# A hybrid GLA and RWKV-7 layer on one core: the input projection by seven block products instead of eight, and the triangular inverses behind it

## The chip, the cores and the metric

The kernel runs on one core of a Trainium2 chip. The core's engines each work through a queue of their own, strictly in order: TensorE (PE in the profile, its weight loads PEld), VectorE (DVE), ScalarE (ACT), GpSimd (POOL) and SyncE (SP), which here only issues DMAs, nearly all of them. The time is the device time of one execution in microseconds (us), the median of the runs of a kernel on the same chip; lower is better.

## The reference, cut to what matters

One encoder layer over 2048 tokens of width 1024, all in float32:

```python
h   = x @ w_in                      # [2048, 1024] @ [1024, 3344]: the input projection
A   = GLA(h[:, :1552])              # q 256, k 256, v 512, gate 512, gate-rank 16
B   = RWKV7(token_shift(h[:, 1552:]))   # r, k, v 512 each, three low-rank inputs 64 + 64 + 128
gates = sigmoid(x @ w_merge + b_merge)  # [2048, 2 * 1024]
mix = (gates[0] * (A @ w_branch[0]) + gates[1] * (B @ w_branch[1])) @ w_out
x   = LN(alpha * x + mix)
x   = LN(alpha * x + relu(x @ W1 + b1)**2 @ W2 + b2)
```

The token shift mixes each projected RWKV column with the same column of the token before: `u + (prev - u) * mu`. GLA and RWKV-7 are recurrences over tokens; the kernel does both in chunks of 128 tokens. For RWKV-7 that takes, for every chunk and head, the inverse of a unit triangular 128x128 matrix, (I - A)^-1 with A made of products of two projected streams, alpha and beta.

## The kernel before, in words

**Stages.** The profiled execution runs through the input projection of the first 1024 tokens (0 to about 432 us), the same of the second 1024 (to about 868 us), 16 chunks of both recurrences (to about 1700 us), the merge and the output product (to about 2200 us) and the MLP (to the end). `HB` is 1024, a "half" of the sequence. A scheduler of the framework decides in which order the recorded instructions stand in each engine's queue: it goes by dependencies and by the order in which the program records them; `high_priority` shifts that.

**Dense products.** float32 is made of two float32r parts, hi (a cast, on ScalarE) and lo (source minus hi, on VectorE or GpSimd; `split`, line 170). Every product is three matmuls, hi by hi, hi by lo, lo by hi (`mm3`, lines 164 to 166). Weights come through four `raw` buffers of 128x1024 (`wslot`, line 155), the load of 512 KB, the cast and the subtraction all ahead of the product.

**Projection of a half** (`phase0`). The input lies in SBUF, channel by token, split (`XH`, `XL`). `gemm` makes 128 features by 1024 tokens from one weight tile: two PSUM tiles of 512 tokens with 8 channel tiles by 3 matmuls each. First come GLA values, one half of the columns token-major (`vpart(1)`: inputs stationary, 264 weight columns moving; the 16 gate-rank columns are among them), then the low-rank inputs, then four rounds j of three gemms (k, r, v of two RWKV heads), each with elementwise work behind it, on POOL the lines 452 (`f`), 465 (`be`) and 472 (`ka`). The log decays stay in SBUF as `lwh`, `lwl`, and a cumulative-sum product per round takes them from there. The products alpha, beta, and others go to DRAM (line 440).

**Inverses** (`tstage`, once per half). It loads alpha and beta of 8 chunks back (line 647), makes A by 64 matmuls (line 654), sends the diagonal 32x32 blocks to DRAM by 32 small DMAs (line 559) and back one block to a partition (`QZ`, line 560), inverts them in 30 steps of two DVE operations (lines 565, 567), sends them out and back (`qe`), transposes (line 669) and puts the 128x128 inverses together by small matmuls (`rwkv_t`). `tstage(h)` stands inside `phase0`, ahead of eight GLA gemms (q, k, gate) and `vpart(0)`, whose matmuls stand in PE's queue among and behind the inverses' own.

**Chunks** (`phase1`). Of each chunk a serial chain of small matmuls and evacuations; the first evacuation of each chunk is `R` (DVE, line 767). The merge gates, `gates(b)` for 512 tokens (16 weight tiles, 384 dense matmuls `pd<-GH,whi` and so on; lines 164 to 166), are recorded after chunks 3, 7, 11 and 15 at a priority by which they fill PE between the chunks' small products. For b > 0, and for b = 0 from the fifth weight tile on, their lo parts are made on POOL.

**MLP.** Its up product already goes by seven block products: sums of weight blocks on POOL (line 1216, `sum<-raw`), their lo parts on DVE (line 174, `wl<-sum,wh`).

## Time and profile before

| | |
|---|---|
| three runs | 3519.4, 3522.22, 3526.28 us |
| median | 3522.22 us |
| the profiled execution: span | 3521.8 us, 51325 instructions |
| PE busy | 95%, 19704 matmuls |
| DVE, ACT, POOL busy | 67%, 39%, 29% |

The profiled execution's span is its whole time as far as the profile shows it, 0.4 us under the median of the runs. The page gives busy times over the whole span; tables by stretch of time (windows) give them per stage, and the timeline gives single instructions with their start and length, and in brackets how long the engine had idled before and what released it.

### The profile page before, as it was taken

The numbers are of one execution on the slowest core, as the hardware profiler recorded it, in microseconds if no ns is written. First come the engines' busy times: TensorE is split into PE (matmuls) and PEld (weight loads), VectorE is DVE, ScalarE is ACT, GpSimd is POOL, SyncE is SP. The second block draws the span as 40 slices with busy tenths as digits, with TensorE's granted clock in tenths as the row PEclk, the third lists the DMA queues.
The fourth block names the chain that finished last, engine by engine and source line by source line (L and its number), as shares of the span: only waits on it lengthen the run. The fifth ranks groups of instructions, "written<-read, shape, count | busy, mean of one in ns | idle before, by whom it ended". The sixth has DMA issues, their size and how long they took to land.

```text
span 3521.8 us, 51325 instructions
## 1 busy us (share of the span) xinstructions
PE 3333.7 (95%) x19704; PEld 2858.3 (81%) x19704; DVE 2353.1 (67%) x3962; ACT 1377.3 (39%) x2504; POOL 1038.5 (29%) x722
## 2 busy tenths in 40 slices
PE   8999999997899999999999979999989999989997
PEld 6777867777778778777899978999978999978886
DVE  4774547556884746542455577677788667789888
ACT  3532444323333323332322235444444444444553
POOL 0120002102344435443233353222243222244333
PEclk8999999998999999999999989999999999999999
DMA  4335523446434434334444433211233221133222
GB/s 149 108 109 161 165 86 124 138 126 198 137 117 136 157 125 162 126 126 158 165 138 144 136 136 124 72 61 60 72 108 132 72 72 57 64 108 138 100 98 79
DMA packets 268438, 417.74 MB, mean 119 GB/s; under 512 B 52476, under 2 KB 163102, under 8 KB 268192
## 3 DMA queue, kind: packets, MB, share of 16 engines
q1 hardware_dynamic: 268192, 414.46, 35.4%
q8 instruction: 155, 2.54, 0.3%
q14 instruction: 91, 0.75, 0.1%
HBM read 310.57 MB, written 103.81 MB: 118 GB/s over the span
## 4 chain that ended last, share of the span: by engine, by line
PE 57%; DVE 13%; DMA 3%; issue 2%; ACT 2%; POOL 2%; SPq 0%; DVEq 0%; POOLq 0%; ACTq 0%
PE pd L166 11%; PE pd L165 11%; PE pd L164 11%; PE pa L164 5%; PE pa L166 5%; PE pa L165 5%; DVE Qz L854 2%; DVE wl L174 2%; DVE hl L174 1%; PE pa L862 1%; PE pa L743 1%; DMA raw<-in_wu 1%; DVE acc L1275 1%; POOL sum L1216 1%; DVE SC L865 1%
## 5 line engine op out<-in xcount | busy, mean ns | idle before, releaser
L1216 POOL TENSOR_TENSOR sum<-raw 128x512 f32<-128x512 f32 x248 | 350.5, 1419 | 891.6 <-DVE wl L174 744.8
L171 ACT CAST whi<-raw 128x1024 fp32r<-128x1024 f32 (+1 forms) x230 | 227.8, 990 | 822.9 <-PE pa L166 410.2
L1275 DVE TENSOR_TENSOR acc<-acc,pa 128x512 f32<-128x512 f32 x480 | 318.8, 681 | 150.2 <-PE pa L166 148.6
L164 PE MATMUL pa<-whi,hh 128*128 128x512 f32 x960 | 376.7, 393 | 12.0 <-DVE acc L1275 10.5
L165 PE MATMUL pa<-wlo,hh 128*128 128x512 f32 x960 | 376.0, 392 | 3.4 <-DVE wlo L174 3.4
L166 PE MATMUL pa<-whi,hl 128*128 128x512 f32 x960 | 375.2, 391 | 0.0
L174 DVE TENSOR_TENSOR wlo<-raw,whi 128x1024 fp32r<-128x1024 f32 (+1 forms) x170 | 204.4, 1202 | 129.1 <-ACT whi L171 102.1
L164 PE MATMUL pd<-XH,whi 128*128 128x512 f32 x704 | 286.2, 406 | 3.6 <-ACT whi L171 3.6
L166 PE MATMUL pd<-XH,wlo 128*128 128x512 f32 x704 | 284.8, 405 | 1.1 <-DVE wlo L174 1.1
L165 PE MATMUL pd<-XL,whi 128*128 128x512 f32 x704 | 283.4, 403 | 0.0
L174 DVE TENSOR_TENSOR wl<-sum,wh 128x512 fp32r<-128x512 f32 x240 | 195.8, 822 | 82.5 <-ACT wh L171 82.4
L164 PEld LDWEIGHTS pa<-whi,hh 128*128 128x128 f32 x960 | 180.7, 188 | 57.0 <-DVE acc L1275 18.6
L165 PE MATMUL pd<-GL,whi 128*128 128x512 f32 x512 | 220.3, 430 | 0.0
L164 PE MATMUL pd<-GH,whi 128*128 128x512 f32 x512 | 218.8, 427 | 0.0
L166 PE MATMUL pd<-GH,wlo 128*128 128x512 f32 x512 | 218.0, 426 | 0.1
L165 PEld LDWEIGHTS pa<-wlo,hh 128*128 128x128 f32 x960 | 181.1, 189 | 40.4 <-DVE wlo L174 4.0
L166 PEld LDWEIGHTS pa<-whi,hl 128*128 128x128 f32 x960 | 180.7, 188 | 38.4
L171 ACT CAST wh<-sum 128x512 fp32r<-128x512 f32 x240 | 148.4, 619 | 151.2 <-PE pd L165 106.0
L174 POOL TENSOR_TENSOR wlo<-raw,whi 128x1024 fp32r<-128x1024 f32 x60 | 152.3, 2538 | 171.4 <-ACT whi L171 171.4
L452 POOL TENSOR_SCALAR f<-th,dv 128x512 f32<-128x512 f32 x16 | 12.3, 770 | 553.5 <-ACT th L450 553.5
L164 PEld LDWEIGHTS pd<-XH,whi 128*128 128x128 f32 x704 | 135.1, 192 | 45.4 <-issue 9.8
L166 PEld LDWEIGHTS pd<-XH,wlo 128*128 128x128 f32 x704 | 135.1, 192 | 36.4 <-issue 2.8
(374 smaller groups left out, 8942.7 us busy)
## 6 DMA issues: line engine op xcount, KB each, us to landing
raw<-in_wu SPq DMA_DIRECT2D x96, 512.0 KB, 4.3
raw<-in_wd SPq DMA_DIRECT2D x96, 512.0 KB, 3.3
raw<-in_wm SPq DMA_DIRECT2D x64, 512.0 KB, 4.2
raw<-in_wf SPq DMA_DIRECT2D x44, 512.0 KB, 4.1
d_gt<-gt SPq DMA_DIRECT2D x64, 256.0 KB, 2.0
gl<-d_gt SPq DMA_DIRECT2D x58, 256.0 KB, 3.0
raw<-in_wv SPq DMA_DIRECT2D x32, 264.0 KB, 3.8
raw<-in_xT SPq DMA_DIRECT2D x16, 512.0 KB, 4.8
```

Source lines behind the costliest of these rows:

```text
L164: nc.tensor.matmul(ps, lhsT=lhs[0], rhs=rhs[0], start=first, stop=False)
L165: nc.tensor.matmul(ps, lhsT=lhs[0], rhs=rhs[1], start=False, stop=False)
L166: nc.tensor.matmul(ps, lhsT=lhs[1], rhs=rhs[0], start=False, stop=last)
L171: nc.scalar.copy(hi, src)
L174: getattr(nc, lo_eng).tensor_tensor(lo, src, hi.bitcast(F32), op=ALU.subtract)
L452: nc.gpsimd.tensor_scalar(f, th, self.ka1(j), self.ka2(j), op0=ALU.mult, op1=ALU.add)
L743: nc.tensor.matmul(both[q][:, j * 128:j * 128 + 128], lhsT=lh[r, j, :], rhs=rr[r, j, :], start=True, stop=True)
L854: nc.vector.tensor_tensor(Qz[r, :, 0:n, hh, :], E[r], q[r].unsqueeze(2).to_broadcast([64, 2, n, 128]), op=ALU.mult)
L862: nc.tensor.matmul(ps[:, j * 128:j * 128 + 128], lhsT=Kt[:, j, l - l0, :], rhs=rhs, start=True, stop=True)
L865: nc.vector.copy_predicated(dst, m, ps.rearrange("p (a n w) -> p a n w", a=4, w=h))
L1216: getattr(self.nc, eng).tensor_tensor(src, block(spec[0]), block(spec[1]), op=spec[2])
L1275: nc.vector.tensor_tensor(a, a, ps, op=ALU.add)
```

## The change

Per half, `phase0` now makes the projection by Strassen's scheme in Winograd's form.

- `load_x(h)` loads all 1024 tokens (16 DMAs of 256 KB) and builds seven input blocks of 4 channel tiles by 512 tokens, each as hi and lo: the quarters B11, B21, B22 and the sums T1 to T4. Per channel tile (four of them) that is 7 casts on ACT, 2 differences and 5 lo parts on DVE, 2 differences and 2 lo parts on POOL. One set of buffers (`XB`) serves both halves.
- `pair(p)` makes two feature tiles by 1024 tokens at a time. Of the two weight tiles' quarters (A11, A12, A21, A22) it forms s1 to s4, splits seven 128x512 blocks, and runs seven products of 4 channel tiles by 3 matmuls, each 512 columns. Outputs leave PSUM through sums with the temporaries p1, p5 and u3 and land in SBUF (`hb`, from which the token shift now reads). On POOL stand s1 to s4, one output, one addition to p5 and five of the seven lo parts: 11 operations of 128x512 for each pair; the lo parts of A12 and S1 and the other outputs are DVE's.
- 13 pairs per half: the low-rank inputs, then per j k with r and v with a GLA q or k tile, then the four gate and the four value tiles of GLA. The values are now feature-major, stored whole to `d_vg` and transposed per chunk by four matmuls and an ACT copy in `gla_prep`.
- The 16 gate-rank columns get 80 matmuls of their own, 512 columns each, over both halves.
- The log decays `lw` go to DRAM (2 MB a half) and come back, 512 KB ahead of each round j; the cumulative sum is one float32 matmul where two float32r ones stood.
- `tstage(h)` leaves `phase0`. `phase1` begins with `tstage(0)`, `gates(0)`, `tstage(1)`, `gates(1)`; the chunks' loop follows, with `gates(2)` after chunk 6 and `gates(3)` after chunk 13. The SBUF pools of weights are closed and opened anew between projection and chunks, and the DMA scratch size is set to 1024.

The diff, cut to its core:

```diff
+            halves("B11")
+            sub("T1", "B12", "B11", nc.vector)
+            halves("B21")
+            sub("T2", "B22", "T1", nc.gpsimd)
+            halves("T2", lo_eng="gpsimd")
+            halves("T1")
+            sub("B12", "B22", "B12", nc.vector)
+            halves("T3", "B12")
+            sub("B21", "T2", "B21", nc.gpsimd)
+            halves("T4", "B21", "gpsimd")
+            halves("B22")
...
-    def gemm(self, src, evac, lo_eng="vector"):
...
+    def pair(self, src, p, put, evs):
...
+        pool = nc.gpsimd
+        halves("A11", a11, "gpsimd")
+        pool.tensor_tensor(s1, a21, a22, op=ALU.add)
+        pool.tensor_tensor(s2, s1, a11, op=ALU.subtract)
+        halves("A12", a12, "vector")
+        p1 = temp("p1", None, prod("A11", "B11"))
+        out(0, 0, prod("A12", "B21"), p1)
+        evs[0](0)
+        halves("S2", s2, "gpsimd")
+        u2 = temp("p1", nc.vector, prod("S2", "T2"), p1, p1)
+        halves("S1", s1, "vector")
+        p5 = temp("p5", None, prod("S1", "T1"))
+        s3 = v3(self.wp.tile([128, 512], F32, tag="wsa", name="wsa", bufs=1))
+        pool.tensor_tensor(s3, a11, a21, op=ALU.subtract)
+        halves("S3", s3, "gpsimd")
+        u3 = temp("u3", nc.vector, prod("S3", "T3"), u2)
+        out(1, 1, u3, p5, eng=pool)
+        pool.tensor_tensor(p5, p5, u2, op=ALU.add)
+        halves("A22", a22, "gpsimd")
+        out(1, 0, u3, prod("A22", "T4"), ALU.subtract)
+        pool.tensor_tensor(s2, a12, s2, op=ALU.subtract)
+        halves("S4", s2, "gpsimd")
+        out(0, 1, prod("S4", "B22"), p5)
...
+        nc.sync.dma_start(sp["lw"][h], lw)
...
+            nc.sync.dma_start(lw, sp["lw"][h][:, :, j * 128:j * 128 + 128])
...
-        self.tstage(h)
...
+        pair(11, values(0), values(1))
+        pair(12, values(2), values(3))
+        if h + 1 < self.S // HB:
+            steps, xl_close = self.load_x(h + 1)
...
+        for h in range(self.S // self.HB):
+            self.tstage(h)
+            self.gates(h)
...
-            if c % 4 == 3:
+            if c in (6, 13):
                 with self.tc.high_priority(offset=0):
-                    self.gates(c // 4)
+                    self.gates(2 + c // 8)
```

Three places show how the order of the instructions moves. First PE, where the first half's inverses begin. In the kernel before, `L654 ... pa<-raw` are the products A of the inverses, and `pd<-XH,whi` and its two neighbours the dense matmuls of the projection:

```order
L418 MATMUL pa<-rkl,cr 128x512
L654 MATMUL pa<-raw 128x128 x12
L164 MATMUL pd<-XH,whi 128x512
L165 MATMUL pd<-XL,whi 128x512
L166 MATMUL pd<-XH,wlo 128x512
L654 MATMUL pa<-raw 128x128 x4
L164 MATMUL pd<-XH,whi 128x512
```

In the changed kernel the last matmuls of the last product of the second half, `pd<-XB22h,wh` and neighbours (block B22 by weight sum S4), stand ahead of the same products A (now line 755), and the merge gates, `pd<-GH,whi` and neighbours, behind them:

```order
L167 MATMUL pd<-XB22h,wh 128x512
L168 MATMUL pd<-XB22l,wh 128x512
L169 MATMUL pd<-XB22h,wl 128x512
L755 MATMUL pa<-raw 128x128 x64
L167 MATMUL pd<-GH,whi 128x512
L168 MATMUL pd<-GL,whi 128x512
L169 MATMUL pd<-GH,wlo 128x512
```

The products A, which stood between matmuls of the projection, now stand alone between the last dense matmul of the projection and the first of the gates. The inverse's later products of the first half stand behind 216 of the 384 matmuls of `gates(0)`; the second half's A stand behind all 384, and its later products behind 185 matmuls of `gates(1)`.

Second SP, at the same place. Before, the small DMAs `qd<-aab` are followed by stores of the projection's results (`d_qT<-gq`) and by its weight loads (`raw<-in_wf`):

```order
L647 DMA raw<-d_be_127 128x4x128
L559 DMA qd_2374<-aab 32x8x32 x19
L560 DMA QZ<-qd_2374 128x1024
L559 DMA qd_2374<-aab 32x8x32 x13
L512 DMA d_qT_150<-gq 128x512
L512 DMA d_qT_151<-gq 128x512
L155 DMA raw<-in_wf 128x1024
L560 DMA QZ<-qd_2374 128x1024
```

After, the 16 loads of alpha and beta stand behind the store of the projection's last output; `raw<-d_be_231` is the last of them, `raw<-in_xT` the gates' input and `raw<-in_wm` their weights:

```order
L748 DMA raw<-d_be_231 128x4x128
L656 DMA qd_6112<-aab 32x8x32 x18
L657 DMA QZ<-qd_6112 128x1024
L656 DMA qd_6112<-aab 32x8x32 x13
L723 DMA raw<-in_xT 128x512 x3
L657 DMA QZ<-qd_6112 128x1024
L723 DMA raw<-in_xT 128x512 x5
L158 DMA raw<-in_wm 128x1024 x6
```

What follows the `qd` DMAs is no longer stores and loads of products that have weights in hand, but the first loads of the products that come next.

Third POOL, in a round j of the projection. Before, the queue holds the elementwise lines of the RWKV tiles alone, six for each round:

```order
L452 TENSOR_SCALAR f<-th,dv 128x512
L472 TENSOR_TENSOR ka<-kp,Ei 128x512
L465 TENSOR_TENSOR be<-be,Ei 128x512
L452 TENSOR_SCALAR f<-th,dv 128x512
L472 TENSOR_TENSOR ka<-kp,Ei 128x512
L465 TENSOR_TENSOR be<-be,Ei 128x512
```

After, 22 operations of the pairs stand among them (line 177: lo parts; 364 and 383: an output and p5; 368, 369, 379, 386: s1 to s4; 536, 550, 556: the elementwise lines):

```order
L364 TENSOR_TENSOR hb<-u_1759,p_1738 128x512
L383 TENSOR_TENSOR p_1738<-p_1738,p_1651 128x512
L177 TENSOR_TENSOR wl<-wsb,wh 128x512
L386 TENSOR_TENSOR wsb<-raw,wsb 128x512
L379 TENSOR_TENSOR wsa<-raw 128x512
L536 TENSOR_SCALAR t_1810<-th,dv 128x512
L177 TENSOR_TENSOR wl<-wsa,wh 128x512
L368 TENSOR_TENSOR wsa<-raw 128x512
L177 TENSOR_TENSOR wl<-raw,wh 128x512
L556 TENSOR_TENSOR o<-kp,Ei 128x512
L550 TENSOR_TENSOR o<-o,Ei 128x512
```

A round's queue on POOL grows from 6 operations to 28, and weights of the next products (line 177) stand behind the elementwise lines of the current ones.

More of the change, by code (lines that the diff above doesn't have):

```diff
@@ new lines, in wraw, with halves, prod, temp @@
+    def wraw(self, src, p):
+        raw = [self.raw() for _ in range(2)]
+        for x in range(2):
+            self.nc.sync.dma_start(raw[x], src[2 * p + x])
+        return [r.rearrange("p (k f) -> p k f", k=8) for r in raw]
+    def pair(self, src, p, put, evs):
+        nc = self.nc
+        raw = self.ahead.pop(0) if self.ahead else self.wraw(src, p)
+        a11, a12, a21, a22 = (raw[a][:, 4 * k:4 * k + 4, :] for a in range(2) for k in range(2))
+        v3 = lambda t: t.rearrange("p (k f) -> p k f", k=4)
+        s1, s2 = (v3(self.wp.tile([128, 512], F32, tag=t, name=t, bufs=1)) for t in ("wsa", "wsb"))
+        W = {}
+        def halves(n, t, lo_eng):
+            hi, lo = (v3(self.wp.tile([128, 512], F32R, tag="w" + x, name="w" + x, bufs=4)) for x in "hl")
+            self.split(t, hi, lo, lo_eng=lo_eng)
+            W[n] = hi, lo
+        def prod(w, x):
+            ps = self.pd()
+            for k in range(4):
+                self.mm3(ps, tuple(t[:, k, :] for t in W[w]), tuple(t[:, k, :] for t in self.XB[x]), k == 0, k == 3)
+            return ps
+        def temp(tag, eng, x, y=None, out=None):
+            t = self.T.tile([128, 512], F32, tag=tag, name=tag, bufs=1) if out is None else out
+            if y is None:
+                nc.scalar.copy(t, x)
+            else:
+                eng.tensor_tensor(t, x, y, op=ALU.add)
+            return t
+        def out(a, b, x, y, op=ALU.add, eng=nc.vector):
+            eng.tensor_tensor(put(a, b), x, y, op=op)
+        pool = nc.gpsimd
[21 more added lines that the diff above has]
+        out(0, 1, prod("S4", "B22"), p5)
+        evs[0](1)
+        evs[1](0)
+        evs[1](1)
@@ L427, in phase0 @@
                 for d in range(2):
-                    for i, part in enumerate((lwh, lwl)):
-                        nc.tensor.matmul(ps[:, d, 0:130], lhsT=part[:, c + d, j * 128:j * 128 + 128], rhs=self.cumM, start=i == 0, stop=i == 1)
+                    nc.tensor.matmul(ps[:, d, 0:130], lhsT=lw[:, c + d, :], rhs=self.cumM, start=True, stop=True)
                 nc.scalar.activation(Ex[:, c:c + 2, :], ps[:, :, 0:129], AF.Exp, scale=-DECAY)
@@ L520, in phase0 @@
-        for j in range(4):
-            def ev_g(n, ps, j=j):
-                t = T.tile([128, 512], F32, tag="gth", name="th")
-                nc.scalar.activation(t, ps, AF.Tanh, scale=0.5)
-                q = T.tile([128, 512], F32, tag="gq", name="gq")
-                nc.vector.scalar_tensor_tensor(q, t, 1.0, ps, op0=ALU.add, op1=ALU.mult)
-                nc.sync.dma_start(sp["ug"][b0 + n][:, j, :], q)
-            gemm(A["wf"][18 + j], ev_g)
-        vpart(0, T, ("gq", "gth"), lambda n: self.load_x(h + 1, 0) if n == 0 and h + 1 < self.S // HB else None)
+        T2, t2close = self.pool(f"p0g_{h}", bufs=2)
@@ new lines, in values, with put @@
+        def values(i):
+            ts = {}
+            def put(b):
+                ts[b] = T2.tile([128, 512], F32, tag="gx", name="gx", bufs=4)
+                return ts[b]
+            return put, lambda n: nc.sync.dma_start(sp["vg"][b0 + n][:, i, :], ts[n])
+        pair(9, gates(0), gates(1))
+        pair(10, gates(2), gates(3))
+        pair(11, values(0), values(1))
+        pair(12, values(2), values(3))
+        if h + 1 < self.S // HB:
+            steps, xl_close = self.load_x(h + 1)
+            for f in steps:
+                f()
+            xl_close()
@@ L529, in phase0 @@
+        t2close()
         tclose()
@@ L828, in gla_prep @@
         ug = self.ld("ug", c, [128, 4, 128], 1)
-        vg = self.ld("vg", c, [128, 512])
+        gv = self.ld("vg", c, [128, 4, 128], 1)
+        pv = self.pa()
+        for j in range(4):
+            nc.tensor.transpose(pv[:, j * 128:j * 128 + 128], gv[:, j, :], self.ident)
+        vg = T.tile([128, 512], F32, tag="vgt", name="vgt", bufs=2)
+        nc.scalar.copy(vg, pv)
         qk = T.tile([128, 2, 128], F32, tag="qk", name="qk", bufs=1)
```

310 lines of the change are left out of this document (151 added, 159 removed).

## The prediction

> **What bounds the kernel now.** I read the page's busy shares and its chain first, then windows by stage. Of the page, the busy line and the chain by engine:
>
> ```profile
> PE 3333.7 (95%) x19704; PEld 2858.3 (81%) x19704; DVE 2353.1 (67%) x3962; ACT 1377.3 (39%) x2504; POOL 1038.5 (29%) x722
> PE 57%; DVE 13%; DMA 3%; issue 2%; ACT 2%; POOL 2%; SPq 0%; DVEq 0%; POOLq 0%; ACTq 0%
> ```
>
> TensorE bounds the whole. The stages that the change touches, as windows (window, its length, then busy time of PE, PEld, DVE, ACT, POOL with counts, granted clock, DMA share, GB/s): the two halves of the projection, the chunks, the start, and the step from projection to chunks.
>
> ```profile
> 0.00:432.00 432.00, 406.94 (x2552) 321.63 (x2553) 250.82 (x378) 170.62 (x312) 39.06 (x37) 0.96 0.44 136
> 432.00:868.00 436.00, 405.13 (x2579) 318.26 (x2578) 258.43 (x400) 167.46 (x315) 56.81 (x49) 0.95 0.44 135
> 868.00:1700.00 832.00, 786.18 (x5055) 657.95 (x5055) 482.08 (x1056) 264.84 (x420) 339.75 (x205) 0.99 0.42 136
> 0.00:44.00 44.00, 32.34 (x206) 30.73 (x207) 21.23 (x37) 18.93 (x27) 0.20 (x4) 0.92 0.73 239
> 836.00:880.00 44.00, 26.73 (x195) 24.45 (x194) 32.76 (x60) 17.23 (x29) 21.45 (x18) 0.77 0.75 232
> ```
>
> The projection loses only 25 and 31 us of PE's time. POOL is nearly free there (39 and 57 us): that slack, and the inverses hidden beside gemms, are what the change spends.
>
> **Matmuls.** Their price is the spacing of starts, since busy times overlap. Timeline of PE, nine matmuls of 512 columns from the first row to the second, six of 264 from the third to the fourth; then the group of the chunks' transposes of values; then two DVE instructions one round j apart:
>
> ```profile
> 202.01 0.39 PE L165 MATMUL pd<-XL,whi 128*128 128x512 f32 x1
> 204.12 0.40 PE L165 MATMUL pd<-XL,whi 128*128 128x512 f32 x1
> 423.90 0.29 PE L166 MATMUL pd<-whi,XL 128*128 128x264 f32 x1
> 424.64 0.29 PE L166 MATMUL pd<-whi,XL 128*128 128x264 f32 x1
> ```
> ```profile
> L732 PE MATMUL pa<-cf,ld_vT 128*128 128x128 f32 x64 | 11.5, 282 | 5.2 <-DMA ld_vT<-d_vT 5.2
> ```
> ```profile
> 179.66 0.17 DVE L432 COPY e<-Ex 128x8 f32<-128x8 f32 x1 [0.23 <-ACT Ex L430]
> 221.89 0.17 DVE L432 COPY e<-Ex 128x8 f32<-128x8 f32 x1 [0.23 <-ACT Ex L430]
> ```
>
> 2.11 / 9 = 0.234 us, 0.74 / 6 = 0.124 us. Before: 2 halves x 22 gemms x 48 = 2112 of the first and 2 x 2 x 192 = 768 of the second. After: 26 pairs x 7 x 12 = 2184, and 80 for the gate ranks. So 2264 - 2112 = 152 more of the first (+35.6) and 768 fewer of the second (-95.2): -60. The values' transposes, 64 of the shape in the group's row, add 11.5; the gate ranks' 16 go, at most a quarter of that: -3. The cumulative sums trade two cheap matmuls for one float32 one: zero, a microsecond or two either way. **PE's work: -52**, certain by the counts; all else is what PE waits.
>
> A round now is 42.2 us: 144 x 0.234 = 33.8, and 8.5 of small products and waits. After, it has 168 dense matmuls: 39.4 + 8.5 = 47.9 (it takes in a GLA tile, so it is longer, not slower).
>
> **The start.** PE's first matmul, and the loads of the input:
>
> ```profile
> 6.30 1.25 PE L164 MATMUL pd<-whi,XH 128*128 128x264 f32 x4 [6.30 <-ACT whi L171]
> ```
> ```profile
> raw<-in_xT SPq DMA_DIRECT2D x32, 256.0 KB, 2.9
> ```
>
> Before, `vpart` starts on quarters of the input, and 44 us lose 44 - 32.3 = 12 us. After, the first pair's last two products need T4 and B22 of all four channel tiles, behind 4 MB of loads and 1 MB of weights (22 us at the window's 239 GB/s) and behind POOL's 16 and DVE's 28 operations on the input, which (next part) largely exclude each other: 16 x 1.31 + 28 x 0.68 = 40 us, beside the pair's own sums. The pair so ends between 50 us (the 40 beside the loads) and 69 (behind them, with the last products), and holds 84 x 0.234 = 20 us of matmuls: 30 to 49 lost, less the 12 lost before: 18 to 37. I take **+20**, near the small end, since each channel tile's operations start when its four loads are there.
>
> **The low-rank part.** Stores and loads of 512 KB land in 4 us:
>
> ```profile
> raw<-in_wm SPq DMA_DIRECT2D x64, 512.0 KB, 4.2
> ```
>
> A 2 MB store, then the first 512 KB back, stand ahead of the first cumulative sum, and PE, in order, waits behind it: some 5 us a half: **+10** for both (0 to 20).
>
> **POOL beside DVE in the rounds.** POOL's elementwise groups, and the MLP's three instructions that show the price, the second started while the first ran, the third alone:
>
> ```profile
> L452 POOL TENSOR_SCALAR f<-th,dv 128x512 f32<-128x512 f32 x16 | 12.3, 770 | 553.5 <-ACT th L450 553.5
> L465 POOL TENSOR_TENSOR be<-be,Ei 128x512 f32<-128x512 f32 x16 | 28.2, 1760 | 4.8 <-issue 4.8
> L472 POOL TENSOR_TENSOR ka<-kp,Ei 128x512 f32<-128x512 f32 x16 | 25.1, 1569 | 26.2 <-DVE kp L454 26.2
> ```
> ```profile
> 2904.67 1.31 POOL L1216 TENSOR_TENSOR sum<-raw 128x512 f32<-128x512 f32 x1 [0.88 <-DMA raw<-in_wu]
> 2905.25 1.28 DVE L174 TENSOR_TENSOR wl<-raw,wh 128x512 fp32r<-128x512 f32 x1 [1.91 <-ACT wh L171]
> 2907.85 0.68 DVE L174 TENSOR_TENSOR wl<-sum,wh 128x512 fp32r<-128x512 f32 x1
> ```
>
> The DVE subtraction takes 0.68 alone; started 0.58 after POOL's sum it ends at 2906.53, 0.55 after POOL's end (2905.98). It got nothing done while POOL read SBUF, but for 0.13 us of entry. So the two queues add up: per round POOL holds 22 x 1.31 + 2 x (0.77 + 1.76 + 1.57) = 37.0 us; DVE has 26 operations with two SBUF inputs (4 lo parts of weights, 22 elementwise ones) of 0.55 to 0.68, 14.3 to 17.7. Together 51.3 to 54.7; I take 53 against PE's 47.9: 5.1 x 8 rounds = **+41**. Bounds: 0 where PE still covers it, 81 where DVE becomes the bound (rival below). The skill's page "SBUF — State Buffer" ("Who interferes with whom") says that a VectorE instruction with two SBUF inputs contends with a GpSimd one that reads SBUF and fully blocks for the whole of it. By that rule every DVE operation costs its full 0.68 behind POOL, the round is 54.7 and the term +54; the trace's 0.55 says somewhat less.
>
> **Between the halves.** The second half's input blocks have one set of buffers: T2, T4 and their lo parts wait on POOL behind the first half's last pair, and the next first product on those. Like the start, but loads come ahead: **+10** (0 to 20).
>
> **The inverses.** SP's queue and PE in the first half's inverses; landing times of the gates' 256 KB and the weights' cast; DVE's steps on `QZ` (the first and the last) and the transposes behind them; the lo parts on POOL; the windows that hold the first and the second half's `qd`:
>
> ```profile
> 272.73 0.63 SPq L647 DMA_DIRECT2D raw<-d_be  x1
> 273.45 11.10 SPq L559 DMA_DIRECT2D qd<-aab  x19
> 285.11 7.09 SPq L559 DMA_DIRECT2D qd<-aab  x13
> ```
> ```profile
> 274.07 3.47 PE L654 MATMUL pa<-raw 64*128 64x128 f32 x32 [0.19 <-ACT aab L655]
> ```
> ```profile
> L171 ACT CAST whi<-raw 128x1024 fp32r<-128x1024 f32 (+1 forms) x230 | 227.8, 990 | 822.9 <-PE pa L166 410.2
> d_gt<-gt SPq DMA_DIRECT2D x64, 256.0 KB, 2.0
> ```
> ```profile
> 306.60 0.26 DVE L565 TENSOR_TENSOR qtmp<-QZ 128x60 f32<-128x60 f32 x1
> 344.01 0.22 DVE L567 TENSOR_TENSOR QZ<-QZ,qtmp 128x60 f32<-128x60 f32 x1
> 358.62 1.30 DVE L669 STREAM_TRANSPOSE tn<-tt 128x512 f32<-128x512 f32 x2
> ```
> ```profile
> L174 POOL TENSOR_TENSOR wlo<-raw,whi 128x1024 fp32r<-128x1024 f32 x60 | 152.3, 2538 | 171.4 <-ACT whi L171 171.4
> ```
> ```profile
> 264.00:308.00 44.00, 39.51 (x206) 32.14 (x207) 5.56 (x10) 11.52 (x20) 0.00 (x0) 0.90 0.72 183
> 704.00:748.00 44.00, 41.52 (x170) 32.72 (x169) 32.41 (x55) 8.02 (x11) 0.00 (x0) 0.96 0.46 155
> ```
>
> Before, these windows lose 4.5 and 2.5 us: gemms with weights in hand ran while SP spent 11.1 + 7.1 = 18.2 us on issuing `qd`. After, nothing dense is in hand. From the last Strassen product to the first gate matmul stand, one after another: the output's store (2.0), 16 loads of alpha and beta (0.63 each: 10) and the last one's landing (2.9), the last A and its copy (1), `qd` (18.2) and its landing, for which SP's `QZ` load waits (2), eight loads of `in_xT` (0.5 each: 4), `in_wm` (4.2) and its cast (1): 45 us, in which PE has 64 products A, 7 us. 38 idle. At the second, the loads of four chunks come ahead and no store is waited for: 45 - 7 = 38, 31 idle. 38 + 31 - 7 = **+62** (50 to 72). Nothing fills it: PE's queue holds A alone between `XB22` and `GH`.
>
> Then the inverse's later products. Before, from the last A (277.5) to the transposes (358.6) went 81 us, the DVE steps 37.6 of them, with POOL at 0.00. After, PE's idle 38 and 216 gate matmuls (51 us) stand against that in the first, 31 and 185 (43) in the second: 8 short at the second, and gate splits now run on DVE, and POOL's lo parts of 2.54 us hold off the steps, whose inputs both lie in SBUF. **+15** for both (0 to 35).
>
> **The chunks.** Their start has now gates beside it: of the window 836 to 880, 17 us idle, go: **-17**. The pace, from `R` of a chunk to the next, with 24 gate matmuls between the first two rows, and 191 between the others:
>
> ```profile
> 945.35 0.68 DVE L767 COPY R<-pa 128x512 f32<-128x512 f32 x1
> 980.01 0.68 DVE L767 COPY R<-pa 128x512 f32<-128x512 f32 x1
> 1062.40 0.69 DVE L767 COPY R<-pa 128x512 f32<-128x512 f32 x1 [4.51 <-PE pa L765]
> 1138.83 0.69 DVE L767 COPY R<-pa 128x512 f32<-128x512 f32 x1 [2.27 <-PE pa L765]
> ```
>
> 34.7 and 76.4 us: (76.4 - 34.7) / 167 = 0.25 a matmul, 0.016 over its price; half of the 1536 gate matmuls leave the chunks and run dense: some **-9** (0 to -12).
>
> **Sum:** -52 + 20 + 10 + 41 + 10 + 62 + 15 - 17 - 9 = **+80**, on 3521.8 (0.4 under the runs' median): **3602 us**. With the port term kept, the other terms' bounds drawn half-way give 3570 to 3635.
>
> **Rivals.**
> *PE hides all that POOL and DVE do* (faster). It decides where POOL's operations hold DVE off for under 1.1 us, or DVE slips between them, so that a round stays within PE's time. Then the port's 41, the 15 of late inverses, 15 of the start's and the 10 between the halves go. Besides, outputs now go through SBUF, so a round could lose its waits of today, which this window, about one round long, shows:
>
> ```profile
> 88.00:132.00 44.00, 40.61 (x184) 31.51 (x184) 32.28 (x39) 28.22 (x47) 7.33 (x6) 0.96 0.24 81
> ```
>
> 3.4 us x 8 = 27. 108 in all: 3522 + 80 - 108 = 3494. For it: DVE is only 59% busy in the projection, and tiles are buffered. Against it: 1.31 in POOL's row, and the 37 of 48 us that POOL alone would fill. 0.20.
> *DVE in its order becomes the bound* (slower still). Its own work in a round, scaled from the projection's 509 us over 868, with the outputs' sums in the evacuations' place, is some 34 us; with waits on POOL's operations and on ACT and PE it could take 58 instead of 53: 5 x 8 = +40: 3642. For it: an in-order queue hardly fills every gap. 0.22.
> *It cancels out*: a port term near zero and the inverses at their small end leave about zero to +20. 0.10, of which 0.06 within 0.2% (7 us, the spread of the three runs, and about what a measurement of this kernel can tell from no change).
> That the change does not do what it says is excluded by the order: 12 matmuls a product, 7 products a pair.
>
> **How the numbers follow.** The forecast has 0.48; slower = 0.48 + 0.22 + 0.04 = 0.74, same 0.06, faster 0.20. The range goes from the first rival, 3490, to 3660, past the second with its own few us.
>
> **What would show it.** Right: PE idle about 38 and 31 us between the last `XB22` and the first `GH`, and between the two blocks of gates; rounds j of 51 to 55 us, with DVE's two-input operations ending 0.55 after POOL's; the first pair ending past 50 us. Wrong: rounds at 48 us or less, or dense matmuls inside the issue of `qd`.

## The result, and the profile after

The changed kernel takes 3686.01 us (median; 3684.01 to 3687.84) against 3524.25 in the same set of runs: 1.046 times as long, 95% interval 1.0444 to 1.0475, or +162 us. The forecast was +80. The profiled execution has a span of 3681.9 us, +160. Of all runs below, one execution, of the kernel with the input blocks on DVE, took 5969.92 us at a granted clock of 0.84; it is left out. The page:

```profile
span 3681.9 us, 50968 instructions
PE 3333.9 (91%) x19136; PEld 2828.4 (77%) x19136; DVE 2559.2 (70%) x4030; ACT 1448.9 (39%) x2672; POOL 1496.5 (41%) x1040
```

PE is busy for as long as before (3333.7), with 568 fewer recorded matmuls; all that is new is waiting, and matmuls that run slowly. The windows that answer to those of before, and then the start, a stretch of three rounds, and the way from the projection to the chunks:

```profile
0.00:432.00 432.00, 360.32 (x1342) 256.84 (x1342) 315.84 (x316) 186.69 (x349) 300.73 (x207) 0.89 0.35 116
432.00:868.00 436.00, 367.11 (x1515) 273.70 (x1516) 267.01 (x303) 169.96 (x311) 242.22 (x175) 0.89 0.38 119
0.00:44.00 44.00, 21.51 (x44) 12.13 (x44) 39.56 (x31) 19.34 (x34) 34.43 (x25) 0.85 0.51 167
158.00:329.00 171.00, 148.54 (x589) 111.06 (x588) 137.26 (x140) 73.48 (x148) 121.86 (x86) 0.92 0.34 114
790.00:1212.00 422.00, 312.00 (x2703) 256.70 (x2702) 195.01 (x299) 137.62 (x242) 123.17 (x81) 0.80 0.54 161
1212.00:1857.00 645.00, 599.95 (x4287) 514.86 (x4286) 457.59 (x1039) 204.16 (x346) 232.79 (x158) 0.97 0.40 126
```

POOL went from 39 to 301 us in the first window. The granted clock (the share of TensorE's full clock that the profile shows) fell from 0.96 to 0.89 there, and is 0.80 between projection and chunks. Four instants divide the execution: the last product of the projection, the first `R` of a chunk, the first product of the merge (`BH,WBh`), the end. In the changed kernel, with the first gate matmul as well:

```profile
790.22 0.40 PE L169 MATMUL pd<-XB22h,wl 128*128 128x512 f32 x1
839.86 0.80 PE L167 MATMUL pd<-GH,whi 128*128 128x512 f32 x1 [27.88 <-ACT whi L174]
1212.03 0.69 DVE L868 COPY R<-pa 128x512 f32<-128x512 f32 x1 [1.52 <-PE pa L866]
1856.82 0.28 PE L167 MATMUL pd<-BH,WBh 128*128 128x256 f32 x1
```

In the kernel before:

```profile
837.90 0.28 PE L166 MATMUL pd<-whi,XL 128*128 128x264 f32 x1
872.13 0.69 DVE L767 COPY R<-pa 128x512 f32<-128x512 f32 x1 [0.52 <-PE pa L765]
1696.95 0.28 PE L164 MATMUL pd<-BH,WBh 128*128 128x256 f32 x1
```

From the merge on both take 1825 us (3521.8 - 1697.0, 3681.9 - 1856.8), so all 160 us arise ahead of it. The two kernels differ there in where the gates and the inverses stand, and that no single trace takes apart; the experiments do.

### The profile page after: what moved, and what is told of

The parts are those of the page before. It is cut to its first block, busy times and chain, and to the rows that moved or that the text cites. A ratio compares the mean times of both kernels' runs of the same rounds, so it can differ in the third digit from the quotient of the medians.

```text
span 3681.9 us, 50968 instructions
## 1 busy us (share of the span) xinstructions
PE 3333.9 (91%) x19136; PEld 2828.4 (77%) x19136; DVE 2559.2 (70%) x4030; ACT 1448.9 (39%) x2672; POOL 1496.5 (41%) x1040
## 4 chain that ended last, share of the span: by engine, by line
PE 55%; DVE 13%; DMA 4%; issue 3%; ACT 2%; POOL 2%; SPq 1%; DVEq 0%; POOLq 0%; ACTq 0%
PE pd L167 10%; PE pd L169 10%; PE pd L168 10%; PE pa L167 5%; PE pa L168 5%; PE pa L169 5%; PE pa L968 1%; DVE wl L177 1%; DMA raw<-in_wu 1%; DVE Qz L960 1%; DVE AK L846 1%; POOL sum L1322 1%; DVE hl L177 1%; DVE rs_t L190 1%; DVE acc L1381 1%
## 5 line engine op out<-in xcount | busy, mean ns | idle before, releaser
L174 ACT CAST whi<-raw 128x1024 fp32r<-128x1024 f32 x154 | 161.5, 1049 | 644.5 <-PE pa L169 394.8
L177 DVE TENSOR_TENSOR wl<-raw,wh 128x512 fp32r<-128x512 f32 x134 | 159.1, 1190 | 29.6 <-ACT wh L174 28.4
L167 PEld LDWEIGHTS pd<-GH,whi 128*128 128x128 f32 x512 | 102.2, 200 | 88.5 <-ACT whi L174 68.1
L174 ACT CAST wh<-raw 128x512 fp32r<-128x512 f32 x186 | 114.3, 616 | 124.7 <-PE pd L168 81.3
L169 PE MATMUL pd<-BH,WBl 128*128 128x256 f32 x512 | 145.0, 283 | 1.2 <-DVE WBl L177 1.2
L1271 ACT ACTIVATE C<-C,pv 128x384 f32<-128x384 f32 (+1 forms) x192 | 110.7, 577 | 88.7 <-DVE C L1270 88.3
L168 PE MATMUL pd<-BL,WBh 128*128 128x256 f32 x512 | 144.9, 283 | 0.0
L177 DVE TENSOR_TENSOR wlo<-raw,whi 128x1024 fp32r<-128x1024 f32 x94 | 120.2, 1279 | 35.5 <-ACT whi L174 35.5
```

The source lines that it names most:

```text
L167: nc.tensor.matmul(ps, lhsT=lhs[0], rhs=rhs[0], start=first, stop=False)
L168: nc.tensor.matmul(ps, lhsT=lhs[0], rhs=rhs[1], start=False, stop=False)
L169: nc.tensor.matmul(ps, lhsT=lhs[1], rhs=rhs[0], start=False, stop=last)
L174: nc.scalar.copy(hi, src)
L177: getattr(nc, lo_eng).tensor_tensor(lo, src, hi.bitcast(F32), op=ALU.subtract)
L1271: nc.scalar.activation(t, t, AF.Relu, bias=self.pv("bup", 2 * p + a))
```

## The experiments

Each was timed in three rounds against the kernel before; "saves" and "costs" below are differences of such ratios, times 3520 us. The interval of each ratio is some 0.002 to either side, 7 us.

### What the inverses cost at either place

Left out: the inverses altogether, with zeros stored in place of their results. In both kernels, in `tstage`, from the products A to the last store:

```diff
-        aab = [[self.rwkv_a(c) for c in range(4 * g, 4 * g + 4)] for g in range(h * n, h * n + n)]
...
-        for g in range(n):
-            self.rwkv_t(h * n + g, aab[g], qe[g])
+        for c in range(h * n * 4, h * n * 4 + n * 4):
+            nc.sync.dma_start(self.sp["YT"][c], self.YT[c % 4])
```

In the changed kernel: 

> The changed kernel without the inverses altogether (no loads of alpha and beta, no products A, no small DMAs, no steps, no later products; zeros are stored in their place). From the last product of the projection to the first chunk it takes 422 us, of which 184 are 786 gate matmuls and some 33 the start of the chunks: if all the rest is the inverses, 205 go: 3481. If the gates by themselves are held up there, by weights that come 512 KB per 5.6 us of products, less: 3520 to 3560.

In the kernel before: 

> The kernel before without the inverses, the same left out. Its PE spends 83 us on their products, and the kernel with the move alone had its projection 24 us shorter beyond that: 3521 - 107 = 3414. With the run without inverses of the changed kernel, the difference of the two savings is what the move costs in the changed kernel; by the run with the move alone it is 82. If the inverses were better hidden in the kernel before than the trace shows, 3440 or more.

And in the changed kernel with the gates recorded ahead of those stores: 

> The changed kernel without the inverses, as before, but with the zeros' stores and the load of the mask left out of the gates' way: the first gates' input is loaded ahead of the zeros. Without the inverses PE still stood 28 us before the first gate matmul, and eight stores of zeros took 8 us of SP's queue there. If the rest is the way from the last product to the first gate by itself (the weights' buffers are opened anew, input, split, weight, cast), some 15 us of idle time stay and the kernel comes to 3516 - 13 = 3503. If it was all the stores, 3490.

Measured: 3515.75 (ratio 0.9991), 3408.73 (0.9686) and 3506.21 us (0.9953, 0.9938 to 0.9968). So the inverses cost 0.0314, 111 us, in the kernel before, near the 107 expected. In the changed one they cost 0.0507, 178 us, by the run with the gates first, or 0.0469, 165 us, by the plain run, in which the stores of zeros stand ahead of the gates' loads. I take the first: that is 68 more (54 by the plain run), and without any inverse the changed kernel is still 0.0267, 94 us, slower. The four instants in those two executions, first of the changed kernel (with gates first), then of the one before:

```profile
792.77 0.40 PE L169 MATMUL pd<-XB22h,wl 128*128 128x512 f32 x1
807.98 0.80 PE L167 MATMUL pd<-GH,whi 128*128 128x512 f32 x1 [14.82 <-ACT whi L174]
1028.03 0.69 DVE L839 COPY R<-pa 128x512 f32<-128x512 f32 x1 [1.29 <-PE pa L837]
1676.21 0.28 PE L167 MATMUL pd<-BH,WBh 128*128 128x256 f32 x1
```
```profile
736.30 0.28 PE L166 MATMUL pd<-whi,XL 128*128 128x264 f32 x1
763.31 0.69 DVE L747 COPY R<-pa 128x512 f32<-128x512 f32 x1 [0.47 <-PE pa L745]
1581.10 0.28 PE L164 MATMUL pd<-BH,WBh 128*128 128x256 f32 x1
```

With the gate matmuls taken out of each stage at 0.234 us (776 of 1536 ahead of the first chunk in the one, 1 in the other; 786 and 0 in the kernels with inverses), in us:

| | projection | to the first chunk | chunks | to the merge, with gates |
|---|---|---|---|---|
| before, no inverses | 736 | 27 | 458 | 1581 |
| changed, no inverses | 793 | 53 | 470 | 1676 |
| before | 838 | 34 | 465 | 1697 |
| changed | 790 | 238 | 469 | 1857 |

So +160 is +56 for the projection by seven products, +27 for the gates' place ahead of the chunks (15 of it the idle stretch in the row at 807.98, which stays even where the gates' loads come first), +12 in the chunks, and +65 for the inverses and the wait around them.

### The move alone

```diff
-        self.tstage(h)
         # --- GLA tiles
...
+        for h in range(self.S // self.HB):
+            self.tstage(h)
+            self.gates(h)
...
-            if c % 4 == 3:
+            if c in (6, 13):
```

The kernel before with this part alone. 

> The kernel before with one part of the change: the inverses and the gates of the first 1024 tokens stand ahead of the chunks, the projection stays as it was. The trace of the changed kernel has, against before, the products A with their idle time at +53 us, the inverse's later products at +38, the gate matmuls among them at +34, the chunks' start at -6 and the rest of the chunks at +4. If the move by itself makes these, about 3524 + 120 = 3645 us. By the terms of the prediction (62 + 15 - 17 - 9) 3575 us. If the excess over the forecast belongs to the projection by seven products, 3530 us or less.

Measured: 3603.9 us, 1.0232 (1.0216 to 1.0248): +82. Neither number. The move gives back more than the trace's sums had it: the projection ends 106 us earlier, 83 of that the inverses' own products, 23 what they had taken from the gemms beside them.

### POOL and DVE in the projection

```diff
-        pool = nc.gpsimd
-        halves("A11", a11, "gpsimd")
+        pool = nc.vector
+        halves("A11", a11, "vector")
...
```

All eleven operations of a pair on DVE. 

> The changed kernel with all eleven operations that a pair had on POOL put on DVE, where one takes 0.68 us instead of 1.31 and needs no port of another. If POOL's operations hold DVE off, a round j falls from 57 us to DVE's own 34 + 22 x 0.68 = 49, and eight of them give -60: 3626 us. If DVE in its own order is what bounds the round, it gets 15 us longer, 72: 3686 + 120 = 3806. If the round is set by neither (PE's small products, waits for PSUM), 3686.

```diff
-            sub("T2", "B22", "T1", nc.gpsimd)
-            halves("T2", lo_eng="gpsimd")
+            sub("T2", "B22", "T1", nc.vector)
+            halves("T2")
...
```

The input blocks' operations on DVE. 

> The changed kernel with the four operations per channel tile that the input's blocks had on POOL put on DVE. The first pair ended at 67 us, and the second half's first pair took 41 us, for 20 us of matmuls each. If POOL and DVE exclude each other there, the 44 operations on DVE alone take 30 us instead of 40 or more: both get 8 to 10 us shorter, 3668 in all. If the loads or ACT's casts set them, 3686; if DVE is the bound there, 3690 to 3700.

Both together. 

> The changed kernel with both the pairs' and the input blocks' operations of POOL on DVE. Alone they gave 36 and 15 us. If both are the port that POOL and DVE share, in different places, they add: 3686 - 51 = 3635. If DVE becomes the bound at the start with both, less: 3650.

Measured: 3650.08 (1.0368, 1.0351 to 1.0386), 3670.39 (1.0416) and 3647.59 us (1.0367): 32, 15 and 33 us saved. Giving DVE eleven more operations per pair makes the kernel faster. A stretch of DVE and of POOL in a round of the changed kernel, the same time in both:

```profile
189.05 1.78 DVE L177 TENSOR_TENSOR wl<-raw,wh 128x512 fp32r<-128x512 f32 x1
190.76 0.68 DVE L364 TENSOR_TENSOR hb<-pd,p 128x512 f32<-128x512 f32 x1
191.36 1.16 DVE L177 TENSOR_TENSOR wl<-wsa,wh 128x512 fp32r<-128x512 f32 x1
192.44 1.78 DVE L419 SCALAR_TENSOR_TENSOR u<-hb,pv,u 128x512 f32<-128x512 f32 x1
```
```profile
188.54 1.74 POOL L383 TENSOR_TENSOR p<-p,p 128x512 f32<-128x512 f32 x1
190.24 1.73 POOL L177 TENSOR_TENSOR wl<-wsb,wh 128x512 fp32r<-128x512 f32 x1
192.05 1.63 POOL L386 TENSOR_TENSOR wsb<-raw,wsb 128x512 f32<-128x512 f32 x1
```

DVE's operations with two SBUF inputs end 0.55 (190.83 after 190.28), 0.55 (192.52 after 191.97) and 0.54 us (194.22 after 193.68) after POOL's, as in the MLP; the one that reads PSUM (`hb<-pd,p`) takes its 0.68. POOL's, 1.28 to 1.31 when alone, are held as well, up to 1.75: the two take turns. With the pair on DVE (a later round of that kernel, at the same work):

```profile
206.36 0.68 DVE L177 TENSOR_TENSOR wl<-wsa,wh 128x512 fp32r<-128x512 f32 x1
207.08 0.69 DVE L379 TENSOR_TENSOR wsa<-raw 128x512 f32<-128x512 f32 x1
207.73 0.75 DVE L419 SCALAR_TENSOR_TENSOR u<-hb,pv,u 128x512 f32<-128x512 f32 x1
```

By the ends of pairs in the two timelines of PE, three rounds take 57.2 us each, and 53.0 with the pair on DVE, where DVE alone is busy 143 of 160 us:

```profile
153.00:313.00 160.00, 146.26 (x589) 110.20 (x589) 142.86 (x202) 73.04 (x147) 21.12 (x18) 0.95 0.34 117
```

So 49 us a round was too good. DVE in its order is the likely bound short of it, but no run shows that. Nor does this run part the two causes that fit it: that POOL's operations hold DVE's, which the rows show, and that POOL's are themselves the slower ones (1.3 us and more ahead of a weight, for 0.68). That the two changes do not add is seen in the ends of pairs: with both, the first pair ends at 55 instead of 67 us (59 with the pairs' alone), but the second and the third take as long as ever.

### The low-rank part

```diff
-            nc.sync.dma_start(lw, sp["lw"][h][:, :, j * 128:j * 128 + 128])
+            nc.sync.dma_start(lw, A["wm"][j].rearrange("p k f -> p k f"))
```

> The changed kernel with each round's load of log decays replaced by a load of the same size of a weight that is in DRAM from the start: it no longer waits for the 2 MB store, and the decays computed with are not the right ones. The prediction priced this wait at 10 us for both halves: 3676. The trace has the second pair 35 us long for 20 us of matmuls in both halves; if the wait for the store and for the stores ahead of the load in SP's queue is that, 3660. If the low-rank products and their evacuations set the end there, 3686.

Measured: 3684.82 us, 1.0465 (1.045 to 1.0481). Not having to wait for the store gains nothing (the store stays, and so does a load of the same size). In PE's timeline the second pair is late by what stands ahead of it in the queue. Of the low-rank products, from PE's timeline of the changed kernel:

```profile
75.51 1.13 PE L472 MATMUL pa<-wup,tw 65*128 65x512 f32 x2
76.57 0.70 PE L475 MATMUL pa<-aup,alow 33*128 33x256 f32 x2
...
82.12 2.08 PE L472 MATMUL pa<-wup,tw 65*128 65x512 f32 x2
84.12 1.22 PE L475 MATMUL pa<-aup,alow 33*128 33x256 f32 x2
```

From 79 us on each takes about twice as long, and nothing dense stands beside them. PE is never idle there. The granted clock is 1.00 from 74 to 78 us and 0.50 from 80 to 94: it halved in the middle of an unbroken row of small products, and the first dense matmuls behind it, to 99 us, still start 0.427 us apart.

### What makes the inverses dear at the new place

Five tries, each at one suspected cause. The gates ahead of the inverses:

```diff
         for h in range(self.S // self.HB):
+            with self.tc.high_priority(offset=0):
+                self.gates(h)
             self.tstage(h)
-            self.gates(h)
```

> The changed kernel, with the gates of each half recorded ahead of the inverses at a shared priority, so that their loads stand ahead of the small DMAs in SP's queue and 307 gate matmuls ahead of the products A in PE's. If the queue order makes the two idle stretches (50 and 41 us around the products A, 91 in all, against 32 in the kernel before), some 59 us go: 3627, and up to 30 more where the inverse's later products now also have gates between them (112 in a row without, instead of 184): 3600. If the latency of the chain of DMAs itself sets the end, or if DVE's steps are what is late, 3670 to 3690.

The small DMAs on POOL's queue:

```diff
-                    nc.sync.dma_start(qd[g, u:u + 8].rearrange("h s t -> s h t"), aab[g][c][q(i), :, q(i)])
-            nc.sync.dma_start(QZ[:, g], qd[g])
+                    nc.gpsimd.dma_start(qd[g, u:u + 8].rearrange("h s t -> s h t"), aab[g][c][q(i), :, q(i)])
+            nc.gpsimd.dma_start(QZ[:, g], qd[g])
```

> The changed kernel with the 64 small DMAs of the diagonal blocks and the loads of QZ issued by POOL's queue instead of SP's. In the changed kernel PE stood 27.9 and 25.6 us between the products A and the first gate matmul, and in the run with the gates first 16.8 and 16.4 us in the middle of the gates, each time until a weight's cast. If SP's 18 us of issue ahead of the weights' loads make these, 35 to 45 us go: 3645. If it is the chain's own latency (loads, products, copies) or weights that come too slowly anyway, 3675 to 3690. POOL's issue could also hold the gates' lo parts, which would give it back.

DVE's steps left out:

```diff
-        for j in range(30, 0, -1):
...
```

> The changed kernel without DVE's 60 steps on QZ in each half (30 times a product and a sum; the blocks go out uninverted). PE has the same products. In the trace the way from the last product of the projection to the first chunk is two chains of an inverse one behind the other, 169 and 167 us, beside which PE has 92 us of gates and 40 of the inverse's own products each. If the length of these chains is what PE waits for, in whatever place of the queue the wait shows, each gets 35 to 40 us shorter and up to 36 of it is PE's wait: 3686 - 65 = 3620. If the waits come from SP's queue, from weights or from the products themselves, the steps cost nothing: 3680 or more. DVE's release of the port could give a few us in either case.

The later products left out, in both kernels:

```diff
     def rwkv_t(self, g, aab, qe):
-        tt4 = T.tile([128, 4, 8, 32], F32, tag="tt4", name="tt4", bufs=2)
...
+        for c in range(4):
+            nc.sync.dma_start(self.sp["YT"][4 * g + c], self.YT[c])
```

> The changed kernel without the inverse's later products: the assembly of the 128x128 inverses with its copies, transposes and loads is left out, and zeros are stored in their place; the products A, the small DMAs and DVE's steps stay. If those products stand uncovered, they cost their 51 us of before and some 72 more: 3686 - 123 = 3563 us. If they were hidden behind gates as the prediction had it (15 for both), 3686 - 66 = 3620. If DVE's steps are what is late, 3650 or more, since they stay.

> The kernel before without the inverse's later products, the same that was left out of the changed kernel, where it saved 85 us. In the trace of before those products take 51 us of PE, between gemms. If they cost PE's time and no more there, 3521 - 51 = 3470. If they were partly hidden or free, 3490 or more. If they cost 85 here too, 3436, and the move has added nothing to them.

The gates' lo parts on DVE:

```diff
-            wh, wl = self.wslot(self.A["wm"][m], lo_eng="gpsimd" if b or m > 3 else "vector")
+            wh, wl = self.wslot(self.A["wm"][m], lo_eng="gpsimd" if b > 1 else "vector")
```

> The changed kernel with the lo parts of the first two blocks of gates on DVE, so that POOL has nothing to do while DVE inverts the diagonal blocks. The prediction had POOL's lo parts of 2.54 us hold off DVE's steps there. If that is what makes the inverses late, 3686 - 25 = 3660. If the length of the steps decides nothing, as leaving them out altogether gained 8 to 13 us, 3686, and with DVE's additional 1.2 us per weight 3690.

Measured: gates first 3692.32 us (1.0485, 1.0464 to 1.0506), the DMAs on POOL 3693.02 (1.0486), no steps 3672.78 (1.0444, 1.0421 to 1.0467), no later products 3600.52 (1.0226) and 3474.42 (0.9867), lo parts on DVE 3668.82 (1.0415, 1.0388 to 1.0442). The waits of over 8 us in PE's timeline of the changed kernel after the row at 839.86, then all such waits with the gates first, then with the DMAs on POOL:

```profile
1024.41 0.80 PE L167 MATMUL pd<-GH,whi 128*128 128x512 f32 x1 [25.57 <-ACT whi L174]
1078.04 0.80 PE L167 MATMUL pd<-GH,whi 128*128 128x512 f32 x1 [10.45 <-ACT whi L174]
```
```profile
803.30 0.79 PE L167 MATMUL pd<-GH,whi 128*128 128x512 f32 x1 [14.36 <-ACT whi L174]
936.95 0.80 PE L167 MATMUL pd<-GH,whi 128*128 128x512 f32 x1 [16.79 <-ACT whi L174]
989.22 0.79 PE L167 MATMUL pd<-GH,whi 128*128 128x512 f32 x1 [8.56 <-ACT whi L174]
1128.45 0.80 PE L167 MATMUL pd<-GH,whi 128*128 128x512 f32 x1 [16.37 <-ACT whi L174]
1180.45 0.80 PE L167 MATMUL pd<-GH,whi 128*128 128x512 f32 x1 [8.54 <-ACT whi L174]
```
```profile
822.97 0.79 PE L167 MATMUL pd<-GH,whi 128*128 128x512 f32 x1 [10.98 <-ACT whi L174]
904.51 0.80 PE L167 MATMUL pd<-GH,whi 128*128 128x512 f32 x1 [9.91 <-ACT gt L731]
1029.60 0.79 PE L167 MATMUL pd<-GH,whi 128*128 128x512 f32 x1 [33.51 <-ACT whi L174]
1089.08 0.79 PE L167 MATMUL pd<-GH,whi 128*128 128x512 f32 x1 [10.48 <-ACT gt L731]
```

Both new orders took away the wait that they aimed at: the first gate matmul comes 37 us earlier with the gates first, and 17 with the DMAs on POOL (803.30 and 822.97 for 839.86). The same time then stands elsewhere. With the DMAs on POOL the later products begin 19 us later (910.6 for 892.0): the 32 DMAs of the first half leave POOL's queue between 800.5 and 839.2, where SP had issued its last at 824.1. And the second wait is 33.5 us for 25.6. The later products cost 47 us in the kernel before (0.0133) and 82 in the changed one (0.0234): 35 of the 65 us. They stand there with nothing between them, 184 and 151 in a row, each step waiting for an evacuation:

```profile
902.82 1.94 PE L806 MATMUL pa<-Tlo,aab 64*64 64x64 f32 x16 [6.17 <-DVE Tlo L800]
936.64 1.11 PE L806 MATMUL pa<-Tlo,aab 64*64 64x64 f32 x16
896.00:928.00 32.00, 19.81 (x271) 17.97 (x265) 13.82 (x25) 12.58 (x29) 2.34 (x1) 0.50 0.36 132
936.00:959.00 23.00, 21.99 (x297) 17.21 (x297) 12.29 (x21) 4.33 (x7) 4.80 (x2) 1.00 0.38 139
```

The first row stands in the bare row, the second a little later, where gates stand between; the windows behind them hold the two (length, busy PE, PEld, DVE, ACT, POOL, granted clock, DMA share, GB/s). In the bare row PE is idle for 12 of 32 us, and the granted clock is 0.50; among gates it is 1.00, and the same 16 records (a float32 product leaves two, so 8 products) take 1.11 us for 1.94. In the kernel before they always stood so, between gemms:

```profile
371.53 1.14 PE L705 MATMUL pa<-Tlo,aab 64*64 64x64 f32 x16
```

PE's busy time tells how much this slow running is. Between projection and first chunk it is 312 us, and 203 without the inverses; less ten gate matmuls the difference is 106, and the inverses' products take 82 in the kernel before. So by this estimate some 24 of the 65 us are products and gates at the lower clock, and the rest is idle time. POOL's lo parts cost 16 of the 65. That the steps seem to cost only 6 proves less than expected: without them the scheduler put 264 later products in a row straight behind A and left 346 gate matmuls alone behind those, so the steps' time was taken by products without cover.

### The gates among the later products, and more of them

```diff
             self.tstage(h)
-            self.gates(h)
+            with self.tc.high_priority(offset=500):
+                self.gates(h)
```

> The changed kernel with the gates recorded at a priority 500 earlier, so that the inverse's later products stand in PE's queue with 3 to 10 gate matmuls between their steps, where 184 and 151 of them stood in a row. The two idle stretches around the products A stay as they are. Leaving those products out saved 85 us in the changed kernel and 48 in the one before. If the 37 us between are the bare row of products, each waiting for the evacuation of the last, most of them go: 3655. If the gates so spread cost as much elsewhere, because DVE, ACT and SP carry both and are what is late, 3686.

With both sets of operations on DVE besides: 

> The pairs' and input blocks' operations on DVE, and the gates interleaved with the inverse's later products. 3648 - 30 = 3618 if the bare row of products is what costs, 3648 if not. Above the kernel before in either case.

```diff
             self.tstage(h)
-            self.gates(h)
+            with self.tc.high_priority(offset=300):
+                self.gates(h)
+        with self.tc.high_priority(offset=300):
+            self.gates(2)
...
-            if c in (6, 13):
+            if c == 11:
```

> The changed kernel with the inverses first as in it, but the gates at a priority that lets them run on into the second half's inverses, and the third block of gates recorded beside the second chain too; the fourth after chunk 11. Between the first chain's end and the second's products A then stand 30 gate matmuls instead of 101, and the second chain has more beside it. If PE waits for the chains' length, the 17 us of gates that stood between the chains move under the second one, and some more from the chunks: 3686 - 30 = 3655. If the gates cost what they cost wherever they stand, as in the run with the gates first, 3686 to 3700.

With the operations on DVE besides: 

> The pairs' and input blocks' operations on DVE, and the gates as in the run with more gates: 3635 - 30 = 3605 if the effects add; 3635 if the gates' place does nothing. Not below the kernel before in either case.

Measured: 3749.92 us (1.0663, 1.0641 to 1.0684), 3714.59 (1.0556), 3692.67 (1.05, 1.0477 to 1.0523) and 3661.79 (1.041): 71 lost, 66 lost against the run with both sets on DVE, 14 lost, 15 lost. Of these guesses only the second one for the run with more gates held (3686 to 3700); the others were wrong. Of the interleaved kernel:

```profile
942.64 0.50 PE L169 MATMUL pd<-GH,wlo 128*128 128x512 f32 x1
943.08 0.24 PE L780 MATMUL pa<-tn,aab 32*32 32x32 f32 x2
943.25 0.50 PE L167 MATMUL pd<-GH,whi 128*128 128x512 f32 x1
...
945.29 0.80 PE L167 MATMUL pd<-GH,whi 128*128 128x512 f32 x1
946.01 0.31 PE L780 MATMUL pa<-tn,aab 32*32 32x32 f32 x2
946.25 0.80 PE L168 MATMUL pd<-GL,whi 128*128 128x512 f32 x1
```

Besides blocks of 3 to 10 gates, the scheduler alternated single gate matmuls with single 32x32 products, 46 times. With the granted clock at 1.00 (942 to 944 us) such a pair takes 0.61 us, where the gate matmul alone takes 0.23 and the product, in a row, 0.03. At 0.50 (945.3 to 950) it takes 0.96, where the two take 0.43 and 0.05. The 46 pairs so cost some 19 us beyond their parts; where the rest of the 71 us comes from is not worked out, but PE's busy time between projection and first chunk grew from 312 to 412 us. So the run says nothing on the bare row: it replaced it by something dearer. No version came below the kernel before; the best of the complete ones is the pairs and input blocks on DVE, 3647.59 us.

## Why the prediction was wrong, point by point

The direction held, and so did the port and the two stretches. The sum was half of the measured one, and no single term holds the difference: the price of the start with its low-rank step and the price of the inverses' later products failed most. In the order of the sum:

- **PE's work, -52.** Right by the counts (2184 and 80 dense matmuls, and 64 transposes in the chunks). But PE is busy as long as before (3333.9 us for 3333.7): matmuls that run slowly take the 52 us back. The sum priced every product at the full clock and had no term for that. In the projection PE is busy 684 us, against 699 in the run with the move alone, with 60 us less of dense work: some 44 us of slow running, which are part of what the next two terms call waiting.
- **The start, the low-rank part and the step between the halves, +20 + 10 + 10.** Up to the first copy of `Ex` the first half waits 81 us beyond its dense matmuls (126.8 - 46.2) against 40 in the run with the move alone, which has the projection of before with no inverses in it (100.8 - 60.4); the second half 56 against 28. That is +68 where 40 stood. The first pair came out inside its bounds (67 us; 50 to 69). What failed is the low-rank step: its price was put on the wait for the store to DRAM, and leaving that wait out gained nothing. The gates' ranks, the low-rank products and the second pair now follow one another with no other dense work at hand, and much of it runs at half speed (granted clock 0.50 from 80 to 94 us). How the 28 us beyond the forecast divide among these no run shows.
- **POOL beside DVE, +41.** Right in kind, a little small: +50 for rounds and the rest of the halves (the projection ends 59 us later than with the move alone and has 60 us less dense work, so it waits 118 more; less the 68), with rounds of 57.2 us for 53, past the forecast's 51 to 55. POOL's operations took 1.4 to 1.7 us, since DVE holds them too; the sum had them at 1.31. The page "SBUF — State Buffer" of the Trainium skill ("Who interferes with whom") has whichever starts first hold the port for the whole instruction: the rows above agree, in both directions, and the 54.7 us a round estimated by it came closer than my 53.
- **The inverses' two stretches, +62.** Right: 49.6 and 41.6 us from the product before to the first gate matmul, for 45 and 38; as the sum has the term, 70 us, inside its bounds of 50 to 72.
- **The inverse's later products, +15, and the chunks' start, -17.** This step failed. It asked only whether DVE's steps end in time, and found gates enough to cover them. It did not count that the products themselves are a chain of some 60 us per half, which stood among gemms and now stands in part bare, at half the clock: that was in PE's order, not in the trace. They cost 82 us where they had cost 47. (A slip in the working, 8 us short at the second half for 81 less 74, changes nothing.) With the gates' own start, inverses and gates together cost +92 (27 + 65) where 62 + 15 - 17 = 60 stood. Putting the stretches right did not gain them, either: they were read as PE's loss, but taking one away only showed the next.
- **The chunks, -9.** Nothing of it: they came out +12, about the transposes' 11.5, which stand in the first term.

The misses are +28, +9, +32 and +9 to +10: some 79 in all. The rival in which DVE becomes the bound gave 3642, and the range ended at 3660. The rounds came most of the way to that rival (57.2 for 58), but it priced them alone. The range was too narrow because every wait was bounded by itself, and all came out at or past the upper part of their bounds together.

What stays open is what sets the length of the stage between projection and chunks. Its price at the new place is settled (178 us against 111), and half of the excess (35) goes with the later products. That the chain of each half, some 168 us from the end of the dense work before it to its last product (790 to 959, 983 to 1150), is longer than the 92 us of gates and 40 of own products beside it fits the trace, but no run varied that length without also changing the order.

## What to carry to other kernels

Work that a gemm hides is not free to move: count the whole chain, its products too, against the work that stands beside it at the new place, in the order and not only in the trace. Small products that are left bare can cost more than the time between them, since the clock was halved there as well. When two engines share a port, price the operations of both as one queue; moving work to the idle engine can make both slower, and moving it back can gain. A wait that is taken away is a gain only if the next one is not right behind it, so leave out the whole of a step once, to learn its price, before mending its parts.

## What the runs showed of the hardware

- Half speed after waits. Dense matmuls of 512 columns start 0.232 us apart, or 0.427. In the changed kernel's projection 148 of them have the longer spacing, against 44 before: 20 us more that no wait shows. The page "TensorE: Matmul & The Clock Gate" of the Trainium skill ("What's actually happening") has the clock halved after an idle window and restored after a busy one; the 0.427 agrees.
- Half speed without a wait. The low-rank products (65x512 and 33x256) halve at 79 us in an unbroken row, with 1.00 granted up to 78 us and 0.50 from 80 to 94. The interleaved kernel's alternating products do so too: PE is never idle from 930 to 960 us, and the granted clock is 1.00 from 942 to 944 and 0.50 from 945.3 to 950. No idle time explains these. Both rows hold products that use a part of the array only; that this is the cause is not shown.
- Alternating a 128x512 matmul with a single 32x32 product costs 0.61 us a pair at a granted clock of 1.00 and 0.96 at 0.50, about twice the two apart (0.26 and 0.48).
- Small DMAs of 32 KB leave POOL's queue more slowly than SP's: 39 us for 32, where SP took 17 for the last 31. The issuing instruction is about as long (0.58 us on POOL, 0.5 to 0.56 on SP); the rest, 20 us, is idle time between them on POOL, up to 2.9 us at a time, for nearly all of which the profile names no cause.
